# Window attention with the probabilities as stationary operand: division by the softmax sum moved from the probabilities to the result

## The chip, the cores and the metric

The kernel runs on one core of one Trainium2 chip. The metric is device time in microseconds (us) of one launch. Engines, as the profile names them: PE is TensorE (matmul), PEld its loading of the stationary operand, DVE is VectorE, ACT is ScalarE, POOL is GpSimd, SP issues DMAs. Each engine takes its own instructions in order; between engines there are semaphores.

## The reference, cut to what matters

Two layers of a hybrid block over 512 latent and 256 context tokens. Each layer mixes tokens in four head groups; the one that matters here is the neighbourhood attention (4 heads of 64), which for 512 latent queries sees a window of 256 keys and all 256 context keys:

```python
s_all = jnp.concatenate([s_win.reshape(s_win.shape[:5] + (nwin,)), s_ctx], axis=-1)
p_all = jax.nn.softmax(s_all, axis=-1)
p_win = p_all[..., :nwin].reshape(s_win.shape)
p_ctx = p_all[..., nwin:]
o = (jnp.einsum("bhrnqwk,bhrwnkd->bhrnqd", p_win, vb)
     + jnp.einsum("bhrnqc,bhcd->bhrnqd", p_ctx, vc))
```

In the first layer the 256 context queries attend to the 256 context keys as well. Everything is float32.

## The kernel before, in words

`na_heads` does the attention of one layer. It loops over two pairs of heads (`pr`), over blocks of 128 queries (`n`: 4 latent ones with 512 keys each; in the first layer 2 more context ones with 256 keys), and over the two heads of the pair (`sub`). One pass of the inner loop is called a unit here, both heads of one block a block-pair: 12 block-pairs in the first layer, 8 in the second, 40 units in all.

A unit computes scores in PSUM (tile `sc`, lines 1199 and 1200), adds the bias table (1208), takes the maximum (1210), exponentiates on ScalarE with the row sum in `sm` (1213), inverts `sm` (1214), scales the probabilities `P` by it (1216 or 1218), transposes them in pieces of 128 keys on TensorE into the PSUM tile `pt` (1221) and copies them to `PT` in SBUF (1223). Then for each block-pair the values `vk` are the stationary operand (64 columns, one head) and `PT` moves through in 128 columns (1230). The result tile `op` has one head in partitions 0 to 63 and the other in 64 to 127, already transposed as the output projection wants it. ScalarE rounds it to `hi` (1238), VectorE takes the rest `lo` (1239).

The tag `pt` has two PSUM buffers, `op` has one. The kernel is built with a tile framework whose scheduler writes out a fixed order of instructions for every engine before the run. It fills the attention with matmuls of `short_conv` (the sub-layer behind it: `L138` to `L140`, tiles `mx` and `mc`, 512 or 256 columns), as far as there are any. At the end of the second layer's attention there are none left.

A float32 matmul stands as two records in the trace, each with its own load of the stationary operand; a transpose, and a matmul of the rounded float32 form in `sc`, `mx` and `mc`, as one.

Of the kernel before, what the change touches and what calls it, by code (L numbers as in the profile page):

```python
# [9 lines left out]
F32 = mybir.dt.float32  # L10
F32R = mybir.dt.float32r
BF16 = mybir.dt.bfloat16
AF = mybir.ActivationFunctionType
OP = mybir.AluOpType
# [31 lines left out]
class Net:  # L46
# [1096 lines left out]
    def na_heads(self, l, src, y, p, pn, with_ctx):  # L1143
        nc, a = self.nc, self.a
        ident = self.c["ident"]
        starts = (0, 8, 24, 32)
        variant = (0, 1, 1, 2)
        deep = 0 if with_ctx else 1
        unit = 0

        for pr in range(2):
            e = T if with_ctx else TX
            vt = p.tile([128, T], F32, name="nav", tag="nav")
            nc.sync.dma_start(vt, src["v", pr])


            qs, ks, kls = [], [], []
            for sub in range(2):
                q = p.tile([128, T], F32R, name="naq", tag=f"naq{sub}")
                k = p.tile([128, T], F32R, name="nak", tag=f"nak{sub}")  # L1160
                kl = p.tile([128, T], F32R, name="nakl", tag=f"nakl{sub}")
                rows = slice(64 * sub, 64 * sub + 64)
                nc.gpsimd.memset(kl[64 - 64 * sub:128 - 64 * sub].bitcast(F32), 0.0)
                nc.sync.dma_start(kl[rows].bitcast(F32), src["k", pr, 1][rows])
                for half in range(2):
                    hr = slice(64 * half, 64 * half + 64)
                    nc.sync.dma_start(q[hr, :e].bitcast(F32), src["q", pr, int(half != sub)][rows, :e])
                    nc.sync.dma_start(k[hr].bitcast(F32), src["k", pr, 0][rows])
                qs.append(q)
                ks.append(k)  # L1170
                kls.append(kl)
            vk = p.tile([128, 10, 128], F32, name="vk", tag="vk")
            for n in range(5):
                if n < 4:
                    vw = p.tile([128, 256], F32, name="vw", tag="nab", bufs=2 + deep)
                    nc.gpsimd.tensor_copy(vw.rearrange("p (r c) -> p r c", c=32),
                                          vt[:, :TX].rearrange("p (r c) -> p r c", c=64)[:, :, starts[n]:starts[n] + 32])
                else:
                    vw = vt[:, TX:]
                pt = pn.tile([128, 2, 128], F32, tag="pt", name="pt", bufs=2)  # L1180
                for kb in range(2):
                    nc.tensor.transpose(pt[:, kb, :], vw[:, kb * 128:(kb + 1) * 128], ident)
                nc.scalar.copy(vk[:, 2 * n:2 * n + 2, :], pt)
            nq = 6 if with_ctx else 4
            for n in range(nq):
                op = pn.tile([128, 128], F32, tag="op", name="op")
                nk = 512 if n < 4 else 256
                PTs = []
                for sub in range(2):
                    h = 2 * pr + sub  # L1190
                    unit += 1
                    if not with_ctx and unit % 3 == 0:
                        sc = self.pm.tile([128, nk], F32, tag="mc", name="sc", bufs=self.mbufs[1])
                    else:
                        sc = pn.tile([128, nk], F32, tag="sc", name="sc", bufs=2)
                    q = qs[sub][:, n * 128:(n + 1) * 128]

                    def score(o, keys):
                        nc.tensor.matmul(o, q, keys(ks[sub]), start=True, stop=False)
                        nc.tensor.matmul(o, q, keys(kls[sub]), start=False, stop=True)  # L1200
                    if n < 4:
                        score(sc[:, 0:256].rearrange("p (r c) -> p r c", c=32),
                              lambda k: k[:, :TX].rearrange("p (r c) -> p r c", c=64)[:, :, starts[n]:starts[n] + 32])
                    score(sc[:, nk - 256:nk], lambda k: k[:, TX:T])
                    if n < 4:
                        bias = p.tile([128, 256], F32, name="nab", tag="nab", bufs=2 + deep)
                        nc.sync.dma_start(bias, a["nab"][l, h, variant[n]])
                        nc.vector.tensor_add(sc[:, 0:256], sc[:, 0:256], bias)
                    mx = p.tile([128, 1], F32, name="mx", tag="mx", bufs=4)
                    nc.vector.tensor_reduce(mx, sc, axis=AX.X, op=OP.max, negate=True)  # L1210
                    P = p.tile([128, nk], F32, name="P", tag="P", bufs=2 + deep)
                    sm = p.tile([128, 1], F32, name="sm", tag="sm", bufs=4)
                    nc.scalar.activation(P, sc, AF.Exp, bias=mx, accum_out=sm)
                    nc.vector.reciprocal(sm, sm)
                    if sub and not with_ctx:
                        nc.vector.tensor_scalar(P, P, sm, None, op0=OP.mult)
                    else:
                        nc.scalar.activation(P, P, AF.Copy, scale=sm)
                    pt = pn.tile([128, nk // 128, 128], F32, tag="pt", name="pt", bufs=2)
                    for kb in range(nk // 128):  # L1220
                        nc.tensor.transpose(pt[:, kb, :], P[:, kb * 128:(kb + 1) * 128], ident)  # L1221
                    PT = p.tile([128, nk // 128, 128], F32, name="PT", tag="PT", bufs=3 + deep)
                    nc.scalar.copy(PT, pt)
                    PTs.append(PT)

                for kb in range(nk // 128):
                    vb = 2 * n + kb if n < 4 and kb < 2 else 8 + kb % 2
                    for sub in range(2):
                        rows = slice(64 * sub, 64 * sub + 64)
                        nc.tensor.matmul(op[rows, :], vk[:, vb, 64 * sub:64 * sub + 64], PTs[sub][:, kb, :],  # L1230
                                         start=kb == 0, stop=kb == nk // 128 - 1)
                hi, lo = y[pr]
                if n < 4:
                    hi, lo = (t[:, :TX].rearrange("p (r n c) -> p n r c", r=8, n=4)[:, n] for t in (hi, lo))
                    op = op.rearrange("p (r c) -> p r c", r=8)
                else:
                    hi, lo = (t[:, n * 128:(n + 1) * 128] for t in (hi, lo))
                nc.scalar.copy(hi, op)
                nc.vector.tensor_sub(lo, op, hi.bitcast(F32))
# [474 lines left out]
```

## Time and profile before

| | us |
|---|---|
| median of 3 runs (1862.79 to 1867.47) | 1864.02 |
| the profiled execution, its own time | 1861.5 |
| its span, first to last instruction | 1859.7 |
| TensorE busy in the span | 1772.7 (95%) |
| VectorE busy | 1267.8 (68%) |
| ScalarE busy | 774.3 (42%) |

The profile is of one execution. A change is worked out against its span, and then set on the median by the difference of the two. TensorE busy times overlap from one matmul to the next, because matmuls are pipelined; what a matmul costs is the distance from its start to the start of the one behind it.

### The profile page before, as it was taken

To read this page: it belongs to the slowest core of one execution; us is meant where nothing else is said; L and a number is where in the kernel's file an instruction comes from. 1 tells how busy PE (TensorE), PEld (TensorE's weight loads), DVE (VectorE), ACT (ScalarE), POOL (GpSimd) and SP (SyncE) were. 2 spreads that over 40 slices of the span, in tenths; PEclk is the share of its full clock that TensorE was granted. 3 is DMA by queue.
4 is the path that set the end of the run, shared out by engine and by line. 5 is a ranking of instruction groups with operands and counts; after the bars stand their busy time and mean duration, and the time that the engine had idled before them with its cause. 6 is when DMAs were issued, how large, how long until landed. Compare 5 with 4: busy or idle time off the path is not lost. (4 is left out here: it accounts for less than half of the span.)

```text
span 1859.7 us, 29504 instructions
## 1 busy us (share of the span) xinstructions
PE 1772.7 (95%) x11170; PEld 1436.0 (77%) x11170; DVE 1267.8 (68%) x2366; ACT 774.3 (42%) x1548; POOL 263.1 (14%) x273
## 2 busy tenths in 40 slices
PE   6899888999999999999999999988899999999998
PEld 2667777788889888888888866777687787777776
DVE  5889898767776777655555586789756765544545
ACT  6333643466565222212222363463347662332323
POOL 0202531600120000000000041162330110000002
PEclk9999999999999999999999999999999999999999
DMA  8452213353565443433444233212235653322322
GB/s 300 150 182 97 91 63 114 118 147 124 182 212 170 146 129 117 123 124 114 130 125 131 83 141 111 69 60 91 73 103 152 210 182 98 106 98 78 115 80 85
DMA packets 105346, 233.55 MB, mean 126 GB/s; under 512 B 13202, under 2 KB 18132, under 8 KB 103925
## 3 DMA queue, kind: packets, MB, share of 16 engines
q1 hardware_dynamic: 105204, 231.68, 38.4%
q8 instruction: 88, 1.44, 0.3%
q14 instruction: 54, 0.43, 0.1%
HBM read 208.42 MB, written 23.21 MB: 125 GB/s over the span
## 5 line engine op out<-in xcount | busy, mean ns | idle before, releaser
L126 ACT CAST whi<-raw 128x512 fp32r<-128x512 f32 x444 | 273.6, 620 | 666.9 <-PE pb L140 269.8
L127 DVE TENSOR_TENSOR wlo<-raw,whi 128x512 fp32r<-128x512 f32 x444 | 317.1, 720 | 216.2 <-ACT whi L126 210.1
L140 PE MATMUL pb<-acth,wlo 128*128 128x512 f32 (+2 forms) x808 | 282.1, 349 | 0.2 <-DVE wlo L127 0.2
L139 PE MATMUL pb<-actl,whi 128*128 128x512 f32 (+2 forms) x808 | 281.8, 349 | 0.0
L138 PE MATMUL pb<-acth,whi 128*128 128x512 f32 (+2 forms) x808 | 280.9, 348 | 0.0
L138 PE MATMUL pb<-whi,hid 128*128 128x512 f32 x628 | 249.7, 398 | 0.8 <-ACT whi L126 0.6
L139 PE MATMUL pb<-wlo,hid 128*128 128x512 f32 x628 | 248.6, 396 | 0.3 <-DVE wlo L127 0.2
L140 PE MATMUL pb<-whi,hid 128*128 128x512 f32 x628 | 248.7, 396 | 0.0
L1498 DVE TENSOR_TENSOR acc<-acc,pb 128x1024 f32<-128x1024 f32 x96 | 117.2, 1221 | 152.6 <-PE pb L140 151.5
L258 DVE SCALAR_TENSOR_TENSOR junk<-adrow,cbc 128x512 bf16<-128x512 f32 x256 | 181.7, 710 | 6.0 <-DMA adrow<-in_adaD_dram 2.9
L139 PE MATMUL mx<-actl,whi 128*128 128x512 f32 x416 | 172.3, 414 | 1.4 <-POOL actl L374 1.2
L140 PE MATMUL mx<-acth,wlo 128*128 128x512 f32 x416 | 171.7, 413 | 0.5 <-DVE wlo L127 0.4
L138 PE MATMUL mx<-acth,whi 128*128 128x512 f32 x416 | 168.8, 406 | 2.1 <-ACT acth L235 1.2
L138 PEld LDWEIGHTS pb<-acth,whi 128*128 128x128 f32 x808 | 152.1, 188 | 20.4
L140 PEld LDWEIGHTS pb<-acth,wlo 128*128 128x128 f32 x808 | 152.0, 188 | 20.1 <-DVE wlo L127 0.4
L139 PEld LDWEIGHTS pb<-actl,whi 128*128 128x128 f32 x808 | 151.8, 188 | 20.1
L374 POOL TENSOR_TENSOR actl<-et,acth 128x256 fp32r<-128x256 f32 (+2 forms) x64 | 56.2, 896 | 732.7 <-DVE et L373 728.5
L138 PEld LDWEIGHTS pb<-whi,hid 128*128 128x128 f32 x628 | 117.8, 188 | 33.0 <-ACT hid L1399 5.4
L140 PEld LDWEIGHTS pb<-whi,hid 128*128 128x128 f32 x628 | 117.8, 188 | 29.5 <-DVE hid L1400 1.8
L139 PEld LDWEIGHTS pb<-wlo,hid 128*128 128x128 f32 x628 | 117.8, 188 | 28.3 <-DVE wlo L127 1.1
L138 PEld LDWEIGHTS mx<-acth,whi 128*128 128x128 f32 x416 | 79.5, 191 | 19.1 <-ACT acth L235 1.6
L139 PEld LDWEIGHTS mx<-actl,whi 128*128 128x128 f32 x416 | 79.7, 192 | 18.3 <-POOL actl L374 1.9
(398 smaller groups left out, 3015.3 us busy)
## 6 DMA issues: line engine op xcount, KB each, us to landing
raw<-in_w_dram SPq DMA_DIRECT2D x276, 256.0 KB, 2.8
adrow<-in_adaD_dram SPq DMA_DIRECT2D x80, 512.0 KB, 3.7
raw<-in_win_dram SPq DMA_DIRECT2D x104, 256.0 KB, 2.6
raw<-in_wout_dram SPq DMA_DIRECT2D x64, 256.0 KB, 3.0
X<-xdr SPq DMA_DIRECT2D x14, 512.0 KB, 4.4
X<-in_xin_dram SPq DMA_DIRECT2D x12, 512.0 KB, 5.1
xdr<-X SPq DMA_DIRECT2D x10, 512.0 KB, 2.8
adp<-in_adaP_dram SPq DMA_DIRECT2D x16, 256.0 KB, 5.5
```

Source lines behind the costliest of these rows:

```text
L126: self.nc.scalar.copy(hi, raw)
L127: self.nc.vector.tensor_sub(lo, raw, hi.bitcast(F32))
L138: mmul(o, st[0], mv[0], start=first, stop=False)
L139: mmul(o, st[0], mv[1], start=False, stop=False)
L140: mmul(o, st[1], mv[0], start=False, stop=last)
L258: nc.vector.scalar_tensor_tensor(self.junk, raw[:, hs], 1.0, self.cbc[:, cnd, hs], op0=OP.mult, op1=OP.mult, accum_out=self.part[:, l, cnd ...
L374: nc.gpsimd.tensor_sub(lo[:, r], t, hi[:, r].bitcast(F32))
L1498: op = nc.vector.tensor_add(o, o, ps)
```

## The change

The exponentials stay undivided. They are transposed and copied as before; then `PT` (128 keys by 128 queries) is the stationary operand and the values of one head move through in 64 columns, so that `op` has queries in its partitions and both heads side by side in its columns. ScalarE divides the first head's 64 columns while it copies them out of PSUM, VectorE the second's, both into the first slab of the first head's `PT`. One transpose of that 128x128 slab on TensorE gives the result in the old layout, in a PSUM tile that takes one of the two `pt` buffers. `hi` and `lo` are made from it as before.

```diff
-                PTs = []
+                PTs, sms = [], []
...
                     nc.scalar.activation(P, sc, AF.Exp, bias=mx, accum_out=sm)
                     nc.vector.reciprocal(sm, sm)
-                    if sub and not with_ctx:
-                        nc.vector.tensor_scalar(P, P, sm, None, op0=OP.mult)
-                    else:
-                        nc.scalar.activation(P, P, AF.Copy, scale=sm)
+                    sms.append(sm)
...
-                for kb in range(nk // 128):
-                    vb = 2 * n + kb if n < 4 and kb < 2 else 8 + kb % 2
-                    for sub in range(2):
-                        rows = slice(64 * sub, 64 * sub + 64)
-                        nc.tensor.matmul(op[rows, :], vk[:, vb, 64 * sub:64 * sub + 64], PTs[sub][:, kb, :],
+                for sub in range(2):
+                    cols = slice(64 * sub, 64 * sub + 64)
+                    for kb in range(nk // 128):
+                        vb = 2 * n + kb if n < 4 and kb < 2 else 8 + kb % 2
+                        nc.tensor.matmul(op[:, cols], PTs[sub][:, kb, :], vk[:, vb, cols],
                                          start=kb == 0, stop=kb == nk // 128 - 1)
+                O = PTs[0][:, 0, :]
+                nc.scalar.activation(O[:, 0:64], op[:, 0:64], AF.Copy, scale=sms[0])
+                nc.vector.tensor_scalar(O[:, 64:128], op[:, 64:128], sms[1], None, op0=OP.mult)
+                op = pn.tile([128, 128], F32, tag="pt", name="oT", bufs=2)
+                nc.tensor.transpose(op, O, ident)
```

In the changed file the lines move: 1218 is now the transposes of `P`, 1220 the copy to `PT`, 1227 the value matmul, 1230 and 1231 the two divisions, 1233 the transpose of the result (tile `oT`), 1240 and 1241 `hi` and `lo`.

Outside the two attention stages no engine's order changes. Inside them the scheduler writes a new one. On TensorE, in the first layer's first pair of heads, the third block-pair stood like this before (operands in the order moving, stationary):

```order
L1221 MATMUL pt<-cst,P 128x128 x4
L1230 MATMUL op<-PT,vk 64x128
L139 MATMUL mx<-actl,whi 128x512
L140 MATMUL mx<-acth,wlo 128x512
L138 MATMUL mc<-acth,whi 128x256
L139 MATMUL mc<-actl,whi 128x256
L1230 MATMUL op<-PT,vk 64x128 x7
L1199 MATMUL sc<-nak,naq 128x256
L1200 MATMUL sc<-nakl,naq 128x256
```

and the same block-pair stands like this now:

```order
L1218 MATMUL pt<-cst,P 128x128 x4
L1227 MATMUL op<-vk,PT 128x64 x4
L1199 MATMUL sc<-nak,naq 128x256
L1200 MATMUL sc<-nakl,naq 128x256
L1199 MATMUL sc<-nak,naq 128x256
L1200 MATMUL sc<-nakl,naq 128x256
L1227 MATMUL op<-vk,PT 128x64 x4
L140 MATMUL mc<-acth,wlo 128x256
L138 MATMUL mx<-acth,whi 128x512
L1199 MATMUL sc<-nak,naq 128x256
L1200 MATMUL sc<-nakl,naq 128x256
L139 MATMUL mx<-actl,whi 128x512
```

The value matmuls stand in two runs of four, one for each head, and the transpose `oT` comes behind 0.9 to 1.5 us of other matmuls in most block-pairs. At the end of the second layer's attention, where no filling matmuls are left, TensorE's order was this before:

```order
L1230 MATMUL op<-PT,vk 64x128 x7
L1221 MATMUL pt<-cst,P 128x128 x5
L1230 MATMUL op<-PT,vk 64x128
L1221 MATMUL pt<-cst,P 128x128 x4
L1230 MATMUL op<-PT,vk 64x128 x7
L1221 MATMUL pt<-cst,P 128x128 x4
L1230 MATMUL op<-PT,vk 64x128
L1108 MATMUL ot<-cst,qtok 128x128 x4
L1230 MATMUL op<-PT,vk 64x128 x7
L1108 MATMUL ot<-cst,qtok 128x128 x4
```

and it is this now:

```order
L1227 MATMUL op<-vk,PT 128x64 x8
L1199 MATMUL sc<-nak,naq 128x256
L1200 MATMUL sc<-nakl,naq 128x256
L1199 MATMUL sc<-nak,naq 128x256
L1200 MATMUL sc<-nakl,naq 128x256
L1233 MATMUL oT<-cst,PT 128x128
L1218 MATMUL pt<-cst,P 128x128 x8
L1227 MATMUL op<-vk,PT 128x64 x8
L1233 MATMUL oT<-cst,PT 128x128
L1218 MATMUL pt<-cst,P 128x128 x8
L1227 MATMUL op<-vk,PT 128x64 x8
L1233 MATMUL oT<-cst,PT 128x128
```

Before, transposes of the next unit stood between the runs of value matmuls; now the last two block-pairs stand strictly one behind the other. ScalarE's order at the same place now:

```order
L1230 ACTIVATE PT<-op,sm 128x64
L1213 ACTIVATE P,sm<-sc,mx 128x512
L1240 CAST ysp<-oT 128x8x16
L1220 COPY PT<-pt 128x512
L1213 ACTIVATE P,sm<-sc,mx 128x512
L1220 COPY PT<-pt 128x512
L1230 ACTIVATE PT<-op,sm 128x64
L1240 CAST ysp<-oT 128x8x16
```

The first division is followed by an exponential (`L1213`) of the last unit but one, and the rounding of the transposed result (`L1240`) queues behind it.

## Rows read from the trace of the kernel before

**Rows 1.** Busy time by engine (PE, PEld, DVE, ACT, POOL) in both attention stretches.

```profile
385.00:458.00 73.00, 72.40 (x523) 58.27 (x522) 51.13 (x140) 53.48 (x132) 3.45 (x6) 1.00 0.46 132
1387.00:1431.00 44.00, 42.53 (x322) 33.29 (x322) 30.26 (x74) 34.34 (x79) 3.42 (x6) 1.00 0.51 148
```

**Rows 2.** TensorE's groups in 385 to 458 us: line, names, stationary, moving, count, busy.

```profile
L1230 PE MATMUL op<-PT,vk 128*64 128x128 f32 x160 | 16.5, 284 | 0.6 <-DVE ysp L1239 0.6
L140 PE MATMUL mx<-acth,wlo 128*128 128x512 f32 x31 | 13.2, 425 | 0.0
...
L1221 PE MATMUL pt<-cst,P 128*128 128x128 f32 x80 | 12.5, 275 | 0.0
L1199 PE MATMUL sc<-nak,naq 128*128 128x256 f32 x36 | 10.2, 304 | 0.0
...
L140 PE MATMUL mc<-acth,wlo 128*128 128x256 f32 x32 | 9.2, 286 | 0.0
```

**Rows 3.** The same groups in the second layer, 1387 to 1431 us.

```profile
L1230 PE MATMUL op<-PT,vk 128*64 128x128 f32 x128 | 12.2, 282 | 0.0
L1221 PE MATMUL pt<-cst,P 128*128 128x128 f32 x64 | 10.4, 282 | 1.5 <-ACT P L1218 1.0 <-DVE P L1216 0.4
L1199 PE MATMUL sc<-nak,naq 128*128 128x256 f32 x28 | 8.0, 307 | 0.0
...
L140 PE MATMUL mx<-acth,wlo 128*128 128x512 f32 x17 | 6.8, 400 | 0.0
```

**Rows 4.** TensorE's timeline over one block-pair: start, duration (us), count of merged records.

```profile
1394.48 0.43 PE L1230 MATMUL op<-PT,vk 128*64 128x128 f32 x2
1394.84 0.51 PE L139 MATMUL mx<-actl,whi 128*128 128x512 f32 x1
1395.18 0.60 PE L1221 MATMUL pt<-cst,P 128*128 128x128 f32 x4
1395.71 1.09 PE L1230 MATMUL op<-PT,vk 128*64 128x128 f32 x14
1396.73 0.39 PE L1199 MATMUL sc<-nak,naq 128*128 128x256 f32 x1
1396.95 0.28 PE L1200 MATMUL sc<-nakl,naq 128*128 128x256 f32 x1
...
1397.31 0.39 PE L140 MATMUL mx<-acth,wlo 128*128 128x512 f32 x1
1397.54 0.39 PE L138 MATMUL mx<-acth,whi 128*128 128x512 f32 x1
```

**Rows 5.** Loads of 128x128 operands before 1 (L478), 24 (L772), 48 (L773) moving columns.

```profile
114.23 0.52 PEld L478 LDWEIGHTS fps<-cst,hn 128*128 128x128 f32 x4 [0.26 <-ACT odd L524]
...
1228.57 0.30 PEld L772 LDWEIGHTS cum<-la,cst 128*128 128x128 f32 x2
1228.79 0.30 PEld L773 LDWEIGHTS cum<-la,cst 128*128 128x128 f32 x2
```

**Rows 6.** The two scalings of `P`: count, duration in ns (least, median, most).

```profile
L1218 ACT ACTIVATE P<-P,sm x32: 499/720/742, 387.5 to 1424.4; 128x512 f32<-128x512 f32 x24, 128x256 f32<-128x256 f32 x8
L1216 DVE TENSOR_SCALAR P<-P,sm x8: 476/480/697, 1393.0 to 1426.6; 128x512 f32<-128x512 f32 x8
```

**Rows 7.** ScalarE's and VectorE's timeline in the second layer's last block-pairs.

```profile
1425.51 0.69 ACT L1213 ACTIVATE P<-sc,mx 128x512 f32<-128x512 f32 x1
1426.09 0.20 ACT L1213 ACTIVATION_READ_ACCUMULATOR P<-sc,mx 128x1 f32 x1
1426.18 0.58 ACT L1223 COPY PT<-pt 128x512 f32<-128x512 f32 x1
...
1426.90 0.27 ACT L1238 CAST ysp<-op 128x128 fp32r<-128x128 f32 x1
...
1427.19 0.29 DVE L1239 TENSOR_TENSOR ysp<-op,ysp 128x128 fp32r<-128x128 f32 x1
```

**Rows 8.** TensorE's timeline: transposes that wait for the scaled `P`.

```profile
1415.61 0.66 PE L1221 MATMUL pt<-cst,P 128*128 128x128 f32 x4 [0.81 <-ACT P L1218]
```

## Prediction

> **What bounds the kernel now.** I read the busy times over the two attention stretches first, since only there does the order of any engine change: 385 to 458 us in the first layer, 1387 to 1431 us in the second. In [rows 1] the reader is to see that TensorE is busy 72.4 of 73 us and 42.5 of 44 us at a granted clock of 1.00, while ScalarE has 53.5 us (73%) and 34.3 us (78%) of work. TensorE sets the end, and work taken from ScalarE is worth only the time in which TensorE waits for it. Second, TensorE's groups by line [rows 2, 3]: how many matmuls of each kind stand there, and the idle time ahead of them. Third, TensorE's own timeline [rows 4], for the price of each kind. A busy time there overlaps with the next, so I take the distance from start to start.
>
> **Prices from start to start.** A filling matmul with 512 columns takes 1397.31 to 1397.54, 0.23 us (0.234 as a mean); one of 256 columns half, 0.118. Fourteen records of L1230 take from 1395.71 to 1396.73, 1.02 us, 0.073 each: two heads sit in different columns of the array and their matmuls overlap. To change to this form and back costs too: four transposes at 0.11 (0.44) ahead of them take 0.53, so 0.09 to enter, and the 256-column matmul behind takes 0.22 for 0.12, so 0.10 to leave. A run of two records takes 1394.48 to 1394.84, 0.36, and 0.34 for the 512-column matmul behind it: 0.36 + 0.09 + 0.11 = 0.56. A run of 14 is 1.21, one of six 0.78 by the same sum.
>
> **Value matmuls before.** TensorE's order has 20 runs of two, 16 of 14 and 4 of six (288 records, 160 and 128 by [rows 2, 3]): 11.2 + 19.4 + 3.1 = 33.7 us. As a check, the stretch less everything else. First layer: 93 matmuls of 512 columns (31 in each of three lines), 96 filling and 72 score matmuls of 256, 80 transposes of P and 22 others: 73 - 21.8 - 19.8 - 11.2 = 20.2. Second layer: 49 of 512, 56 scores of 256, 64 + 25 transposes: 44 - 11.5 - 6.6 - 9.8 = 16.1. Together 36.3, so about 2.6 us of it are waits; the views name 0.6 and 1.5 of them [rows 2, 3].
>
> **Value matmuls after.** Again 288 records, but each has a full 128x128 operand to load and moves only 64 columns. No row of this kernel has this shape. The nearest are full loads with few columns behind them [rows 5]: four for L478 (one moving column) take 0.52 where one takes 0.19, so steps of 0.11, and two for L772 (24 columns) take 1228.57 to 1228.79, 0.11 each. The step is the same for 1 and 24 columns as the 0.11 of a 128x128 transpose, so it is the load that sets it, and moving half as many columns gives nothing. I take 0.112: 288 x 0.112 = 32.3 us. The new form is that of its neighbours, so I charge no change of form. Twenty transposes `oT` add 20 x 0.11 = 2.2. Together 34.5 against 33.7: the matmuls alone cost 0.8 us.
>
> The Trainium skill ("TensorE: Matmul & The Clock Gate", Back-to-back issue gap) gives N/2.4 + 2.5 ns for an isolated matmul of N columns, about 29 ns for 64 and 56 for 128; it adds that this leaves out the load and is too low at small N. By the formula alone 288 x 0.029 = 8.4 us would be left; [rows 5] show the load's price, with which the caveat agrees, and the formula's halving is kept only as a rival.
>
> **ScalarE and VectorE.** Off come 24 scalings of 0.72 us and 8 of 0.50 from ScalarE, 21.3 us, and 8 of 0.48 from VectorE, 3.8 us [rows 6]. On come 20 divisions of 128x64 each. The trace has none of that size; between a 128x1 read (0.20) and a 128x128 copy (0.27 and 0.29) [rows 7] I take 0.2, so 4 us on each engine (at the upper bound 5.8). The 17 us less on ScalarE are not on the path: they lie beside TensorE's work. What can be won there is the wait for the scaled P, 0.81 at 1415.61 [rows 8] and others within the 2.6. I count all 2.6 as gone and charge the new waits in full. No DMA moves past another, since bias loads stay with their units.
>
> **The way back of the result.** Now the result must go from the last value matmul through ScalarE's division, VectorE's division (it writes the same tile, and the scheduler lets it wait for ScalarE), the transpose and `hi` and `lo`. The `oT` transpose takes a `pt` buffer, so the second set of four transposes behind it waits until `lo` has been read. Where matmuls fill in, TensorE has 0.94 to 1.5 us of other work ahead of `oT`, by the orders and the prices above. The chain up to it is 0.16 (a matmul's end comes that much later than the next one's start: 0.28 for a step of 0.12 in [rows 4]) + 0.04 + 0.20 + 0.03 + 0.20 + 0.05 = 0.68 (0.04 and so on are gaps between engines, 0.03 to 0.05 as I read them). It is hidden unless ScalarE is just in an exponential (0.69 + 0.20 [rows 7]). A wait that ends late also exposes one load, 0.11. For these 16 block-pairs I take 0.12 each, 2.0 us; the ends are 0 and, with half of an exponential ahead of most, 0.5.
>
> **The end of the second layer.** There nothing fills in, and the order is: eight transposes, eight value matmuls, `oT`, again. TensorE's work in a block-pair is 8 x 0.11 + 16 x 0.112 + 0.11 = 2.78. The cycle from one `oT` to the next: its end to `hi` (0.27) and `lo` (0.29) with gaps 0.95; second four transposes 0.70 with the exposed load; copy to PT 0.04 + 0.59 + 0.05; second four value matmuls' eight records 1.16; divisions 0.04 + 0.23 + 0.25: 4.0 us. So 1.24 of wait in a cycle, and about 0.7 more from the second to the third block-pair, where an exponential (0.69 + 0.20) stands ahead of `hi` in ScalarE's queue: 1.9. With 0.4 at the start, 0.4 from the first to the second pair and 0.5 at the output transposes behind: 1.24 + 1.9 + 1.3 = 4.4 us.
>
> **Sum.** 34.5 + 2.0 + 4.4 = 40.9 against 36.3: 4.6 us more. The span goes from 1859.7 to 1864.3; the profiled execution's own time lies 1.8 above its span (1861.5), so 1866.1. The median of the runs shown is 2.5 above that execution, which gives 1868.5.
>
> **Rivals.** (1) The way back waits everywhere. `oT` holds a `pt` buffer in each block-pair and both engines take their work in order, with ScalarE three quarters busy; at 0.5 instead of 0.12 in the 16 covered pairs it is 16 x 0.4 = 6.4 more, 1875. For it: exponentials of 0.89 come twice in each block-pair. Against: ScalarE is 17 us lighter. (2) The 64 columns set the step. At 0.056 a record 288 save 16.1 from the 32.3: 1852; with TensorE then waiting more in the uncovered cycles, 1852 to 1857. Against: the steps of [rows 5]. (3) The lighter ScalarE covers the new waits. If the tail loses 2.2 rather than 4.4 and the rest nothing, 4.2 of the 4.6 go: 1864.4, no difference. For it: P is ready 0.7 us sooner in each unit. Against: the tail's order is strictly serial. This rival becomes a gain only if the tail too has no wait (36.3 - 34.5 = 1.8 less, 1862.2); a gain over the measurement's limit therefore needs rival 2, or value matmuls below 0.10 a record, where 288 x 0.012 = 3.5 more are saved.
>
> **How the numbers follow.** A measurement of this kernel can tell about 0.3%, 5.6 us, from no change. The forecast case, matmuls at 0.11, waits mainly at the end of the second layer, has a chance of 0.50 and spans 1866 to 1871.5; since +5.6 (1869.6) lies in it, about 0.33 of it is "same" and 0.17 slower. Rival 1 has 0.27, slower but for 0.02. Rival 3 has 0.15, nearly all same. Rival 2 has 0.08, all faster. That is faster 0.08, same 0.50, slower 0.42. The range leaves out rival 2 and the far end of rival 1: 1860 (no waits at all, and 0.105 a record: 1862.2 less 2.0) to 1876.
>
> **What would show it right or wrong.** In the trace after: steps between L1227 records of 0.11 (right) or 0.06 (rival 2); waits ahead of L1233 and of the L1218 and L1227 behind it, about 1.2 us in each of the last block-pairs and near 0.1 elsewhere (right), or 0.5 elsewhere (rival 1); no wait left for P; divisions of 0.2 us. From 0.12 + 1.0/16 = 0.18 us of mean wait in the 16 covered pairs on, the whole passes +5.6. The prediction falls if the new form costs a change after all (40 runs of it at 0.1 would be 4 us), if the two heads' runs of four overlap in some way that no row shows, or if the order around the attention lets the 4.6 us be made up later in work that TensorE does not bound.

## Result, and the profile after

| | before | changed |
|---|---|---|
| median of 8 runs each, us | 1863.77 | 1874.55 |
| ratio, with 95% interval | | 1.0063 (1.0049 to 1.0077) |
| profiled execution: span, us | 1859.7 | 1877.0 |
| mean granted clock of TensorE | 0.986 | 0.982 |

The change costs about 11 us. The forecast was 4.6 us more (1868.5); its range held the time, and the time lies where one of the rivals, not the forecast, had put it. By the prediction's own limit (0.3%, 5.6 us) the outcome is slower, to which it gave 0.42; it gave 0.50 to no difference.

The profiled executions are 17.3 us apart. To see which part of that is the change, I follow the same matmul through both traces, since TensorE's order outside the attention is the same. The last one ahead of the first attention stage starts at 388.1 before and 394.2 now: 6.1 us were lost where nothing had changed, and executions of one kernel differ so much (1870.8 to 1879.6). From there to 100 us behind the first stage 2.0 are added, from the head of the second stage to 130 us behind it 8.6. These two, 10.6, I take as the change's. In a second profile of the changed kernel (below) they are 5.1 and 8.0. A single stretch is no surer than about 1 us: the first layer of a kernel whose order is the old one up to 1405 us (below, fewer fillers) is 0.9 shorter there than before.

TensorE's price for the new value matmuls is in its timeline (start, duration, merged records):

```profile
1408.98 1.00 PE L1227 MATMUL op<-vk,PT 128*128 128x64 f32 x8
1409.79 0.48 PE L140 MATMUL mx<-acth,wlo 128*128 128x512 f32 x1
1410.11 0.39 PE L138 MATMUL mx<-acth,whi 128*128 128x512 f32 x1
```

From 1408.98 to 1410.11 stand eight records and one 512-column matmul: 1.13 - 0.23 = 0.90, 0.112 each, with nothing for the change of form. Against [rows 4], a run of two is now cheaper (0.22 for 0.56) and a run of 14 dearer (1.57 for 1.21).

What TensorE waits for in the second attention stage, by line and releaser (sum, times, longest):

```profile
PE pt L1218 <- ACT P L1213: 2.9, 1, 2.9
PE oT L1233 <- DVE PT L1231: 2.3, 3, 0.8
PE pt L1218 <- DVE ysp L1241: 0.5, 2, 0.2
PE ot L1108 <- DVE ysp L1241: 0.2, 1, 0.2
```

and in the first layer, 390 to 480 us:

```profile
PE frps L293 <- ACT frow L295: 1.7, 1, 1.7
```

The waits for P scaled [rows 8] are gone. Only 3 of 20 transposes `oT` are waited for. The largest wait, 2.9, is one for an exponential. The timeline shows where:

```profile
1418.81 1.00 PE L1227 MATMUL op<-vk,PT 128*128 128x64 f32 x8
...
1423.83 0.40 PE L140 MATMUL mx<-acth,wlo 128*128 128x512 f32 x1
1427.09 0.66 PE L1218 MATMUL pt<-cst,P 128*128 128x128 f32 x4 [2.85 <-ACT P L1213]
...
1430.41 1.80 PE L1227 MATMUL op<-vk,PT 128*128 128x64 f32 x8
1431.97 0.56 PE L1199 MATMUL sc<-nak,naq 128*128 128x256 f32 x1
```

This is the crossing from the first pair of heads to the second. At 1423.83 the last filler is used, and the next P is ready at 1427. The eight value matmuls at 1430.41 take 1.56 to the next start instead of 0.81. The windows (busy time of PE, PEld, DVE, ACT, POOL, then granted clock, DMA share, GB/s) say why:

```profile
1420.00:1425.00 5.00, 4.23 (x28) 3.26 (x26) 2.00 (x5) 3.24 (x9) 0.40 (x1) 1.00 0.29 83
1425.00:1430.00 5.00, 2.92 (x19) 2.69 (x20) 3.49 (x9) 3.30 (x8) 0.00 (x0) 0.88 0.58 177
1430.00:1435.00 5.00, 5.00 (x25) 5.00 (x25) 2.77 (x9) 1.25 (x4) 0.00 (x0) 0.50 0.13 43
1435.00:1440.00 5.00, 4.29 (x34) 3.93 (x33) 3.72 (x10) 3.79 (x10) 0.00 (x0) 0.94 0.47 139
```

Behind the wait the granted clock falls to 0.50, 1.2 instead of 2.4 GHz; before, it was 1.00 throughout [rows 1]. From 1428.42 to 1435.70, 7.3 us pass for matmuls that take 4.0 at full clock.

The exponential itself comes late, because the bias table that is added to the scores does. Before, its load is issued 0.7 us after the start of the first pair's last value matmul (1408.20):

```profile
1408.91 1.61 SPq L1207 DMA_DIRECT2D nab<-in_nab_dram  x3
```

Now it is 2.6 us after it (1419.53), and the bias add (DVE) and the exponential (ACT) follow from there:

```profile
1420.63 0.29 PE L1233 MATMUL oT<-cst,PT 128*128 128x128 f32 x1
1422.11 0.80 SPq L1207 DMA_DIRECT2D nab<-in_nab_dram  x2
1424.87 0.76 DVE L1208 TENSOR_TENSOR sc<-sc,nab 128x256 f32<-128x256 f32 x2
1426.25 0.69 ACT L1213 ACTIVATE P<-sc,mx 128x512 f32<-128x512 f32 x1 [1.60 <-DVE mx L1210]
```

What the DMA queue waits for there is L1182, the transposes of the second pair's values:

```profile
SPq L1207 <- PE pt L1182: 7.9, 1, 7.9
```

In the kernel their input `vw` shares its buffers with the bias tables (tag `nab`), and their output shares the two `pt` buffers with `oT`. Before, the first of them starts 1.5 us ahead of the last value matmul; now it starts 1.2 us behind it, next after `oT`. The end of the stage:

```profile
1439.31 0.33 PE L1233 MATMUL oT<-cst,PT 128*128 128x128 f32 x1 [0.71 <-DVE PT L1231]
1439.48 0.60 PE L1218 MATMUL pt<-cst,P 128*128 128x128 f32 x4
1440.32 0.65 PE L1218 MATMUL pt<-cst,P 128*128 128x128 f32 x4 [0.24 <-DVE ysp L1241]
1440.81 2.20 PE L1227 MATMUL op<-vk,PT 128*128 128x64 f32 x16
1443.80 0.33 PE L1233 MATMUL oT<-cst,PT 128*128 128x128 f32 x1 [0.79 <-DVE PT L1231]
```

From one `oT` to the next it is 4.49 us here and 4.22 for the following one; the forecast had 4.0.

The second stage, from a matmul just ahead of it to one just behind, adds up as follows (waits are what steps between starts have beyond the prices above, where it is over 0.13; 0.7 of the 8.3 are three steps at half clock):

| us | before | changed |
|---|---|---|
| whole stretch | 61.5 | 71.8 |
| value matmuls and `oT` | 14.8 | 15.2 |
| waits | 2.0 | 8.3 |
| half clock and small remainders | | 3.7 |
| all other matmuls at full clock | 44.6 | 44.6 |

The value matmuls before are what is left of the stretch, so small remainders there are in them. Of the 10.3 us, 1.7 are won back within 130 us behind.

### The profile page after: what moved, and what is told of

It is laid out like the page before. It is cut to its first block, busy times and chain, and to the rows that moved or that the text cites. A ratio compares the mean times of both kernels' runs of the same rounds, so it can differ in the third digit from the quotient of the medians.

```text
span 1877.0 us, 29528 instructions
## 1 busy us (share of the span) xinstructions
PE 1783.2 (95%) x11190; PEld 1455.7 (78%) x11190; DVE 1271.1 (68%) x2378; ACT 763.6 (41%) x1536; POOL 264.1 (14%) x273
## 5 line engine op out<-in xcount | busy, mean ns | idle before, releaser
L138 PEld LDWEIGHTS mx<-acth,whi 128*128 128x128 f32 x416 | 80.1, 193 | 18.8 <-ACT acth L235 1.6
L140 PEld LDWEIGHTS mx<-acth,wlo 128*128 128x128 f32 x416 | 80.2, 193 | 17.8 <-DVE wlo L127 1.3
```

The source lines that it names most:

```text
L138: mmul(o, st[0], mv[0], start=first, stop=False)
L140: mmul(o, st[1], mv[0], start=False, stop=last)
```

## Experiments

Four explanations were to be told apart. Theory A: filling matmuls are a fixed stock. In most block-pairs they now cover the division and `oT`, and then they lack where the stage can't do without, at the crossing and at its end. Theory B: the new form of the value matmuls. Theory C: `oT` in one of two `pt` buffers. Theory D: the division itself. A theory E came up on the way: the half clock was an accident of the first profile. All were timed against the kernel before on the same chip.

| kernel | ratio to before, 95% interval | fillers between the pairs (second layer) | waits there, us | bias load there, us |
|---|---|---|---|---|
| before | 1 | 16 | 0.8 | 0.7 |
| changed, again | 1.0065 (1.0046 to 1.0084) | 9 | 2.9 | 2.6 |
| new layout, P scaled | 1.0065 (1.0043 to 1.0087) | 1 | 4.1 | 2.9 |
| 128 columns moved | 1.0055 (1.0038 to 1.0072) | 14 | 1.2 | 2.6 |
| 12 more matmuls | 1.0045 (1.0029 to 1.0062) | 20 | none | 2.6 |
| result transposed later | 1.0036 (1.0023 to 1.0049) | 17 | none | 1.0 |
| `oT` in `op` | 1.0030 (1.0017 to 1.0043) | 17 | none | 1.6 |
| no way back | 1.0021 (1.0005 to 1.0037) | 19 | none | 0.6 |
| `oT` in `op`, one division | 1.0007 (0.9993 to 1.0020) | 16 | none | 0.6 |
| before, fewer fillers | 0.9997 (0.9983 to 1.0010) | 0 | 3.7 | 0.7 |
| before, unscaled | 0.9974 (0.9960 to 0.9987) | 21 | none | 0.7 |
| before, scaling moved | 0.9988 (0.9973 to 1.0003) | 16 | 1.4 | 0.7 |

Fillers are 512-column matmuls that start between the first pair's last value matmul and the second's first. "None" is no wait over 0.3 us there. The bias load is the issue of the second pair's first one, counted from the start of the first pair's last value matmul. The crossing, up to the second pair's first value matmul, takes 7.2 to 10.1 us (9.4 before, 8.9 changed; only with one filler and P scaled 11.3).

**The changed kernel once more.**

> The changed kernel as it is, once more, beside the others and with a second profile. Theory A: 1872 to 1877 us, and again a wait of 2 to 4 us ahead of the second layer's second head pair (first transposes of P), with a granted clock of 0.50 for some microseconds behind it. If that half clock was an accident of the first profile (theory E), the wait is there and the clock stays at 1.00.

Measured: 1.0065. The wait is the same to the digit; the clock falls too, but later, at the end of the stage:

```profile
PE pt L1218 <- ACT P L1213: 2.9, 1, 2.9
PE oT L1233 <- DVE PT L1231: 2.3, 3, 0.8
```

```profile
1420.00:1425.00 5.00, 2.15 (x16) 1.57 (x14) 4.02 (x10) 3.22 (x8) 0.00 (x0) 1.00 0.59 186
1440.00:1445.00 5.00, 3.98 (x26) 3.61 (x24) 2.58 (x5) 1.83 (x5) 0.00 (x0) 0.78 0.00 0
1445.00:1450.00 5.00, 5.00 (x21) 4.04 (x20) 3.28 (x5) 3.27 (x7) 0.00 (x0) 0.88 0.08 24
```

It costs 1.2 us with small remainders here, 3.7 in the first profile. Here it falls behind the waits at the stage's end, 3.0 us of the last 11. So the wait belongs to the order; that the clock falls somewhere behind the waits was seen twice, where it falls is not fixed. Theory E fails as it was put, and A's place for the drop too. The stage costs 8.0 us more than before (8.6 in the first profile).

**No way back.** Both divisions and the transpose are left out.

```diff
-                O = PTs[0][:, 0, :]
-                nc.scalar.activation(O[:, 0:64], op[:, 0:64], AF.Copy, scale=sms[0])
-                nc.vector.tensor_scalar(O[:, 64:128], op[:, 64:128], sms[1], None, op0=OP.mult)
-                op = pn.tile([128, 128], F32, tag="pt", name="oT", bufs=2)
-                nc.tensor.transpose(op, O, ident)
```

> This kernel leaves out both divisions and the transpose of the result, 20 times each; the rounding reads the undivided result straight from its PSUM tile. Theory A (the changed kernel loses its time where no filling matmuls stand: the way back of the result is covered with filling matmuls in most block-pairs, these are a fixed stock, and the stock is short at the change of head pairs and at the end of the second layer's attention): in the order there are 13 or more 512-column fillers again before the second head pair's first transposes, and nothing between the last block-pairs, so 1860 to 1865 us, no more than 2 us from the kernel before, and value matmuls at 0.11 a record. Theory B (the new form of the value matmuls costs the time): only the 20 transposes go, 20 x 0.11 = 2.2 us, so 1871 to 1873.

Measured: 1.0021, about 4 us above the kernel before and 8 below the changed one. The way back carries two thirds of the net loss, so B fails as the whole cause. But A's number was 0 to 2, and this is more: the time, 1870.1, lies above A's 1860 to 1865 and just below B's 1871 to 1873 (the kernel before took 1865.8 beside it). Compared with the kernel before unscaled (0.9974), which differs from this one only in the form and order of the value matmuls, the new form and order are 0.5% behind, some 8 us, as much as the way back. In the net loss the relief of the next experiment, 5 us, hides part of it. The prices don't explain this: they give 32.3 us for the one and 31.4 for the other. About 4 us of it are in the profiled executions, 2.0 in the first stage and 1.8 in the second. Value matmuls wait for copies of PT for 1.2 in the second stage, but for 0.9 in the unscaled kernel too; the rest I can't place.

**Before, unscaled.** The 40 scalings are left out and nothing is put in their place.

```diff
-                    if sub and not with_ctx:
-                        nc.vector.tensor_scalar(P, P, sm, None, op0=OP.mult)
-                    else:
-                        nc.scalar.activation(P, P, AF.Copy, scale=sm)
```

> The kernel before with the 40 scalings of P left out and nothing in their place: the whole relief that the change gives ScalarE and VectorE, without its layout. Theory A, and the prediction: ScalarE is not what sets the end, so at most the 2.6 us of waits now there, 1861 to 1864. If the relief were worth its busy time (21 us on ScalarE), 1845 to 1855.

Measured: 0.9974, 5 us (2.4 to 7.5). All that the change takes from ScalarE and VectorE, 21 and 4 us of busy time, is worth this. The 2.6 us of waits lie in that interval. In the profile the two stages are 2.1 us shorter in all. The value matmuls also stand in fewer and longer runs in this order (35 instead of 40), which by the prices of the prediction is 2.3 us, so how much the waits are worth is not shown.

**New layout, P scaled.** The division stays on P, the result is copied where the changed kernel divides.

```diff
-                    sms.append(sm)
+                    if sub and not with_ctx:
+                        nc.vector.tensor_scalar(P, P, sm, None, op0=OP.mult)
+                    else:
+                        nc.scalar.activation(P, P, AF.Copy, scale=sm)
...
-                nc.scalar.activation(O[:, 0:64], op[:, 0:64], AF.Copy, scale=sms[0])
-                nc.vector.tensor_scalar(O[:, 64:128], op[:, 64:128], sms[1], None, op0=OP.mult)
+                nc.scalar.activation(O[:, 0:64], op[:, 0:64], AF.Copy)
+                nc.vector.tensor_copy(O[:, 64:128], op[:, 64:128])
```

> The new layout alone: P is divided as in the kernel before, and the result is only copied where the changed kernel divides it. Theory A: the way back is the same and the order has still fewer fillers at the change of head pairs (2), so as slow as the changed kernel or slower, 1873 to 1880. If moving the division were what costs (theory D), this would come back to the kernel before, 1862 to 1867.

Measured: 1.0065. D fails: the loss comes with the layout and its way back. One filler is left at the crossing, and the clock falls behind it again (0.78 from 1430 to 1435 us).

**The result transposed later.** `oT`, `hi` and `lo` of a block-pair (`finish` makes them) stand behind the next block-pair's transposes.

```diff
+                if prev is not None:
+                    finish(*prev)
                 for sub in range(2):
                     cols = slice(64 * sub, 64 * sub + 64)
...
-                op = pn.tile([128, 128], F32, tag="pt", name="oT", bufs=2)
-                nc.tensor.transpose(op, O, ident)
+                prev = (pr, n, O)
```

> All of the changed kernel's work, but the transpose of a block-pair's result and its rounding stand behind the next block-pair's transposes of P. Theory A: the next block-pair's own work now covers the division, so the fillers stay for the change of head pairs (17 of 512 columns there in the order, 9 in the changed kernel) and the tail has transposes between: 1863 to 1867 us, 7 to 11 faster than the changed kernel, with no wait over 1 us ahead of the second head pair's first transposes. Theory B: no gain, 1873 to 1876. Theory C (the transposed result takes one of two transposition buffers and that makes waits in every block-pair): the buffer is still taken 20 times, and later, so no gain or a loss, 1873 to 1880.

Measured: 1.0036, less than half of the loss won back. The mechanism is there. The stage's waits are down to

```profile
PE oT L1154 <- DVE PT L1246: 0.8, 1, 0.8
PE pt L1231 <- ACT P L1226: 0.7, 1, 0.7
PE ot L1108 <- DVE ysp L1162: 0.2, 1, 0.2
PE op L1242 <- ACT PT L1233: 0.2, 1, 0.2
```

with 17 fillers at the crossing, and at the stage's end this kernel is 2.5 us behind the kernel before, the changed one 10.3. `oT` still takes its `pt` buffer, so C fails as an effect in every block-pair. At the crossing it does not fail: there `oT` now comes 9.6 us after the last value matmul, behind the second pair's first ones, and the bias load is issued at 1.0 instead of 2.6. So this run takes away the spent cover and the held buffer together. A's number failed: in the profiled execution another 3.8 us go in the 130 us behind the stage, where TensorE waits for weights (once 1.4 us, at 1524) and the clock is 0.69 for 5 us. Whether every execution has that, one profile doesn't show.

**The transposed result in `op`.** It frees both `pt` buffers for P.

```diff
-                op = pn.tile([128, 128], F32, tag="op", name="op")
+                opp = pn.tile([128, 2, 128], F32, tag="op", name="op")
+                op = opp[:, 0, :]
...
-                op = pn.tile([128, 128], F32, tag="pt", name="oT", bufs=2)
+                op = opp[:, 1, :]
```

> The changed kernel with the transposed result in the second half of the tile op instead of in a transposition buffer. Both buffers now serve P alone, so that the transposes of the next block-pair cover the division; in the order they stand ahead of the result's transpose nearly everywhere, the tail included, and 14 fillers stand at the change of head pairs. Theory C (the buffer makes the waits) and theory A (the cover is what counts) both expect a gain here: 1863 to 1868 us, about that of the kernel that leaves the way back out. Theory B (the form of the value matmuls) expects none: 1872 to 1877.

Measured: 1.0030, 6 us less than the changed kernel: B is refuted as the main cause of the net loss. The second stage is 3.9 us behind the kernel before at its end and 1.5 us 130 us later (the changed kernel 10.3 and 8.6). A and C both expected a gain, so this run doesn't part them. The numbers expected (1863 to 1868) were too low by 3 to 8.

**One division.** On top of that, VectorE divides both heads in one instruction.

```diff
-                    sm = p.tile([128, 1], F32, name="sm", tag="sm", bufs=4)
+                    if sub == 0:
+                        sm2 = p.tile([128, 2], F32, name="sm", tag="sm", bufs=4)
+                    sm = sm2[:, sub:sub + 1]
...
-                nc.scalar.activation(O[:, 0:64], op[:, 0:64], AF.Copy, scale=sms[0])
-                nc.vector.tensor_scalar(O[:, 64:128], op[:, 64:128], sms[1], None, op0=OP.mult)
+                nc.vector.tensor_tensor(O.rearrange("p (s d) -> p s d", s=2), op.rearrange("p (s d) -> p s d", s=2),
+                                        sm2[:, :, None].to_broadcast([128, 2, 64]), op=OP.mult)
```

> The kernel with the transposed result in the second half of op, and the two divisions made one: VectorE divides all 128 columns in one instruction, so that ScalarE, whose queue holds the exponentials, no longer stands in the way back. Theory A: the cover needed shrinks again, 18 fillers at the crossing and 3 left for the tail: 2 to 4 us less than with the transposed result in op alone, ratio to the kernel before 1.000 to 1.002. If the way back's length no longer matters there: the same as without it, 1.003.

Measured: 1.0007 (0.9993 to 1.0020). With the layout kept, no loss is left that these runs can tell; the second stage's waits are

```profile
PE op L1236 <- DVE PT L1233: 0.4, 1, 0.4
PE op L1230 <- DVE ysp L1244: 0.3, 1, 0.3
```

It is no faster than the kernel before, and by the ratios some 6 us slower than the unscaled one (0.9974).

**12 more matmuls at the crossing.**

```diff
+                    if not with_ctx and pr and n == 0 and sub == 1:
+                        warm = pn.tile([128, 512], F32, tag="op", name="warm")
+                        for i in range(12):
+                            nc.tensor.matmul(warm, qs[0][:, 0:128], ks[0][:, 0:512], start=True, stop=True)
```

> The changed kernel with 12 more 512-column matmuls (2.8 us) whose result nobody reads, put at the second layer's change of head pairs, where the changed kernel's TensorE stood still for 3 us and then ran at half clock. Theory A: the added work lies in the wait and the half clock behind it (3.2 us in the changed kernel's profile) is gone: 1869 to 1873 us, granted clock 1.00 from 1420 to 1440 us. If the wait and the clock have nothing to do with each other (theory E), the added work costs up to 2.8: 1874 to 1878.

Measured: 1.0045; the median, 1874.48, lies at the lower edge of E's range. In the profile the wait is gone and the clock stays at 1.00, and with 2.8 us of work added the stage costs 6.4 us more than before instead of 8.0 and 8.6. So added work that nobody needs cost less than nothing in this execution; by the times alone E is not excluded.

**128 columns moved.**

```diff
-                op = pn.tile([128, 128], F32, tag="op", name="op")
+                op = pn.tile([128, 2, 128], F32, tag="op", name="op")
...
-                        nc.tensor.matmul(op[:, cols], PTs[sub][:, kb, :], vk[:, vb, cols],
+                        nc.tensor.matmul(op[:, sub, :], PTs[sub][:, kb, :], vk[:, vb, :],
```

> The changed kernel with twice the columns moved in every value matmul: all 128 value columns, both heads' instead of one's; the halves that nobody reads are computed for nothing. If the load of the stationary operand sets the price (the prediction), a record stays at 0.11 and the time stays that of the changed kernel, or up to 6 us below it, since 13 fillers stand at the change of head pairs in its order instead of 5: 1867 to 1877. If columns set it (0.056 us for 64), 288 x 0.056 = 16 us more: 1888 to 1892.

Measured: 1.0055; the time, 1876.1, is 12 to 16 us below what a price by columns would give. TensorE's timeline:

```profile
1406.80 1.06 PE L1226 MATMUL op<-vk,PT 128*128 128x128 f32 x8
1407.62 0.48 PE L140 MATMUL mx<-acth,wlo 128*128 128x512 f32 x1
1407.93 0.39 PE L138 MATMUL mx<-acth,whi 128*128 128x512 f32 x1
```

Eight records and a 512-column matmul in 1.13, as with 64 columns: 0.112 a record. At the crossing 14 fillers leave 1.2 of the 2.9 us, with the bias load as late as in the changed kernel, so the cover does count there. The time hardly follows, as one `oT` of the first layer waits 2.2 us here.

**Before, with fewer fillers.** 18 of the last 24 filling matmuls of the second layer are left out.

```diff
-            pss = self.big(w_in[cb], hx, segs)
+            pss = self.big(w_in[cb], hx, segs, (0, 4) if l and cb else range(KB))
...
-                for k in range(h0, h0 + 4):
+                for k in [k for k in range(h0, h0 + 4) if k in ks]:
```

> The kernel before, with its old layout and its scaling, and 18 of the 24 last filling matmuls of the second layer left out (18 x 0.234 = 4.2 us of TensorE work; the weights are loaded and split as before). No filler then stands between the two head pairs, where the kernel before has 16. Theory A (fillers are a stock, and the crossing from one head pair to the next takes 8 to 9 us whatever stands in it): the work that is left out turns into a wait of 4 to 5 us at the crossing, likely with half clock behind it, so the time stays or gets longer: ratio 0.999 to 1.003. If fillers were only work on the bounding engine: 4.2 us less, ratio 0.9977.

Measured: 0.9997; a gain of 4.2 us (0.9977) is outside the interval. In the old layout, the stock short at the crossing makes the same picture, waits and then half clock:

```profile
1410.39 0.38 PE L1199 MATMUL sc<-nak,naq 128*128 128x256 f32 x1 [1.60 <-ACT P L1213]
...
1412.97 0.71 PE L1221 MATMUL pt<-cst,P 128*128 128x128 f32 x4 [1.84 <-ACT P L1218]
```

```profile
1405.00:1410.00 5.00, 3.33 (x30) 2.39 (x26) 3.11 (x8) 2.32 (x7) 0.29 (x1) 1.00 0.42 124
1410.00:1415.00 5.00, 2.77 (x14) 2.33 (x15) 4.39 (x12) 4.28 (x11) 0.00 (x0) 0.84 0.81 252
1415.00:1420.00 5.00, 5.00 (x40) 4.09 (x38) 2.92 (x8) 3.40 (x9) 0.00 (x0) 0.81 0.34 100
```

**Before, with scalings moved to VectorE in the first layer too.**

```diff
-                    if sub and not with_ctx:
+                    if sub:
```

> The kernel before with every second scaling of the first layer, too, on VectorE instead of ScalarE (0.48 instead of 0.72 us). TensorE's order is the same but for one place. With ScalarE not on the path nothing changes, ratio 0.999 to 1.001; if waits for the scaled P were worth more in the first layer than the trace names, up to 2 us less, 0.999.

Measured: 0.9988, with 1 inside the interval: not settled.

## Why the prediction was right or wrong, by its steps

**Right: the price of the matmuls.** 0.112 a record was taken and measured, with no charge for the change of form; at that price value matmuls with `oT` come to 19.2 us in the first stage against 18.8, in the second to 15.2 against 14.8. So 0.8 us more, as forecast. That this is all the new form and order cost is not shown: against the unscaled kernel they cost some 8 us, of which the price accounts for 0.9. Rival 2 is out, by the row and by the 128 columns. The Trainium skill ("TensorE: Matmul & The Clock Gate", Back-to-back issue gap) gives N/2.4 + 2.5 ns for an isolated matmul of N columns, by my estimate 29 ns for 64, and says that this leaves out the load and counts too little where columns are few. The trace agrees with that caveat: a record takes 0.112 us whether it moves 64 columns or 128.

**Right: the end of the second layer.** Waits there were put at 4.4 us. They are the 2.3, 0.5 and 0.2 of the view, and one load exposed behind each, 4.0 by the steps. Each cycle is 0.2 to 0.5 longer than worked out, and the larger wait put down to an exponential ahead of `hi` is not there.

**Right: ScalarE's relief sets no end.** 21 us of its work are worth 5 us with nothing in their place, and the changed kernel loses more than that.

**Mis-sized: the divisions.** Taken as 0.2 us, they are, by the groups of the second stage,

```profile
L1230 ACT ACTIVATE PT<-op,sm 128x64 f32<-128x64 f32 x8 | 2.5, 315 | 8.6 <-PE op L1227 7.7 <-ACT whi L126 0.9
L1231 DVE TENSOR_SCALAR PT<-op,sm 128x64 f32<-128x64 f32 x8 | 2.3, 282 | 9.9 <-ACT PT L1230 9.9
```

ScalarE's 0.32 is above the upper bound, the 0.27 of a copy of twice the size [rows 7].

**Wrong: the step on the way back.** The prediction said of 16 block-pairs that TensorE "has 0.94 to 1.5 us of other work ahead of `oT`" and that the chain "is hidden". It is: none of the 16 has a wait in the view (one of 0.4 us in the second profile), less than the 2.0 us booked. But it booked that cover as free. It is made of fillers, and each layer has a fixed number of them: what stands ahead of `oT` is missing later. The new order, known before the run, could have told it, by counting the fillers at the crossing, 16 before and 9 after. The wait there grew from 0.8 [rows 8] to 2.9; the prediction listed that wait among those that go, and its sum has at most the 0.4 "at the start" for it. That a shorter stock makes such a wait is shown in the old layout by leaving fillers out.

The same step has a second fault. "No DMA moves past another" was said of the bias loads, but at the crossing `oT` now stands ahead of them through two shared buffers, and the first is issued at 2.6 instead of 0.7 us. Weight loads (`raw`), too, which followed it before (from 1410.62), now stand ahead of it (from 1412.66). Seven fillers are 1.6 us of cover, the later load is 1.9. The three kernels that don't need the cover (the result later, `oT` in `op`, no way back) have 17 or more fillers there and no long wait, but an earlier bias load as well (1.0, 1.6, 0.6). So that the way back makes the long wait is shown; which of its two effects makes how much is not.

**Missing: the clock.** The prediction took 1.00 throughout from [rows 1]. A stretch in which TensorE stands still was charged with its own length; in both profiles of the changed kernel and in two others with a long wait (P scaled, fewer fillers) half clock came behind, for up to 3.3 us of lost time.

**The rival at 1875.** It has the measured time and the wrong reason: it put 0.4 us more into each of 16 block-pairs, by the `pt` buffer and the engines' queues, and there the trace has nothing; the buffer counts only at the crossing and at the stage's end. The part on what would show it right or wrong named this sign, so the trace decides between the two where the time can't. The range's upper end, 1876, was there for this rival, so that it held the time is luck as far as the mechanism goes.

What remains open is most of the new layout's 0.5% over the unscaled kernel, and the first stage. Right behind it the changed kernel is 3.7 us behind (4.0 in the second profile), and 100 us later 2.0 (5.1). 1.5 us of the 3.7 are a longer wait ahead of L293, 1.7 for 0.2. No experiment was made for it, but the traces fit the account of the fillers: between the last value matmul and L293 stand 6 of 512 columns where there were 11, and every kernel with 9 or more there waits 0.5 or less.

## What to carry to other kernels

Work that hides a latency is spent when it is used. Before a new latency is booked as covered, count the cover: how much filling work the stage has, and what will stand in the places that used it until now. Look also at which buffers the new work holds and what waits for them; here it was the next loads. Where the stock is short, look for cover that the stage makes itself (here the next block's transposes, once the result had a buffer of its own) or shorten the chain (one division instead of two in line): together they took away all of the loss that can be told.

## What the runs showed that was not expected

TensorE's granted clock went to 0.50 inside a stage that is otherwise nearly fully busy, in one execution of the changed kernel right behind a wait of 2.9 us, in another about 20 us later, behind the waits at the stage's end. A 128x64 division out of PSUM took ScalarE 0.32 us, longer than its 0.27 for a 128x128 copy out of PSUM in [rows 7]. And 288 matmul records that move 128 columns took no longer than 288 that move 64.
